# Weight loads move from SyncE's queue to GpSimd's, GpSimd's compute to VectorE: a hybrid attention and RWKV-7 decoder step

## The chip, the cores and the metric

One NeuronCore of a Trainium2 chip runs the whole program in one launch. The metric is the device time of one execution in microseconds (us); three executions of the kernel before took 3533.83, 3536.41 and 3536.74 us, and their median, 3536.41 us, is the time that the change is compared with.

Engine names as in the profile: PE is TensorE, PEld its weight loads, DVE is VectorE, ACT is ScalarE, POOL is GpSimd, SP is SyncE. SP does no arithmetic here: it only issues DMAs, one after another, each when the semaphores that it waits for have come.

## The reference, cut to what matters

One decoder layer (DEPTH is 1) and a final norm, for a prompt of 2048 tokens and for 8 samples of 8 new tokens with a cache of 2048 keys and values each. All inputs are float32, the model width is 1024.

```python
sh1, sc1, gt1, sh2, sc2, gt2 = ada_modulation(c, w_ada, b_ada)
h = rms_norm(x, norm1_g) * (1.0 + sc1) + sh1
proj = h @ w_in                               # 1024 -> 3*512 + 1792 columns
# first 1536 columns: q, k, v of 8 heads; dilated sliding windows (128,1), (512,4), (2048,16)
# other 1792 columns: token shift and low-rank parts, then the RWKV-7 recurrence of 8 heads
mix = concat([att, rw], -1) @ w_out           # 1024 -> 1024
x = x + gt1 * mix
h2 = rms_norm(x, norm2_g) * (1.0 + sc2) + sh2
x = x + gt2 * (square(relu(h2 @ w_ff1)) @ w_ff2)   # 1024 -> 4096 -> 1024
y = rms_norm(x, normf_g)
```

The outputs are y of both groups, the new keys and values, the RWKV states and the last projected rows.

## The kernel before

**Products.** Every large product is made in three passes (`mm3`, L311): weights and activations are each split into a high part, rounded to the matmul's type, and a rest (`split`, L256: ACT writes the high part on L258, DVE the rest on L259), and PE accumulates high times high, high times rest and rest times high in one PSUM tile.

**Weights.** A weight block of 512 KB is loaded into a staging tile named `stg`, split from there into a high and a low tile, and used by PE. `w_in` (L327) makes two such loads for each of 52 blocks of the input projection; `wload` (L1317) makes one for each block of the output projection (`w_out`) and of the feed-forward (`w_ff1`, `w_ff2`). The pools hold two `stg` tiles (three in the pool of the last token group), so a load can start only when the split of the load two before it has ended. Two other loads use the same `stg` tiles: parts of `w_ada` during the second stage (`ada_load`, L210) and the attention output that is read back from DRAM (`mlp_mix`, L1336). Every one of these loads is issued by SP.

**Stages.** The prompt is cut in four windows of 512 tokens. For each there is an input projection (i0 to i3, `in_stage`), an RWKV window (r0 to r3, `rwkv_window`) and an attention window (a0 to a3, `att_load`, `att_scores`, `att_values`); the samples have their own (s). Then five token groups go through output projection and feed-forward (m, p, f). Projections and feed-forward are dense PE work; the RWKV and attention windows are chains of small steps, and the kernel lets the two kinds run beside each other.

**Order.** A planner orders the instructions: `ORDER` (L37) gives each stage a start and an end in planned microseconds, from which each instruction gets a priority, and a scheduler with a cost model (`PlanCosts`, L1613) simulates the engines and fixes the order on each engine's queue. On the chip each queue then runs strictly in that order, and an instruction that has to wait holds up all that stands behind it on its queue.

**RWKV.** For each of 16 chunks of 128 tokens (and once for the samples) `rw_solve` (L676) inverts small triangular matrices. It goes through DRAM twice: `dA` is written (L687), read back into `sol` (L695), solved by DVE on L703 and L709, written as `dT` (L712), and read back in pieces (L716, L720, L721), all on SP. POOL clears `sol` before (L696 to L699). `rw_chunk` (L746) carries the state on: POOL multiplies the old state by the decay (L770), DVE adds the new part (L790, L791). The decay factors `DC` are picked out of `Dt` by six small POOL copies for each chunk (L862), and by two for the samples (L1166).

**Cached keys.** `att_load` (L920) reads queries and keys back from DRAM (`qt`, L934, on SP), transposes and splits them. From the second window on it also loads the transposed keys of the earlier windows from `kTd` into `kT`, which has one buffer (L931, POOL's queue: 12 loads, four for each window, of 512, 1024 and 1536 KB).

What else is on POOL's queue: one load of a constant (L466) and small constants at the start. Apart from L931 and L466 every DMA of the kernel is on SP.

Of the kernel before, what the change touches and what calls it, by code (L numbers as in the profile page):

```python
# [9 lines left out]
F32 = mybir.dt.float32  # L10
# [3 lines left out]
ALU = mybir.AluOpType  # L14
# [108 lines left out]
class Step:  # L123
# [203 lines left out]
    def w_in(self, c0, G):  # L327
        nc = self.nc
        tag = f"w{self.nwb % 2}"
        self.nwb += 1  # L330
        lo = G.tile([128, KD, 256], F32R, name="wlo", tag=tag)
        hi = G.tile([128, KD, 256], F32R, name="whi", tag=tag)
        for h in range(2):
            sl = slice(128 * h, 128 * h + 128)
            sg = G.tile([128, KD, 128], F32, name="stg", tag="stg")
            src = self.I["w_in"][0][:, c0 + 128 * h:c0 + 128 * h + 128]
            nc.sync.dma_start(sg, src.rearrange("(k p) c -> p k c", p=128))
            self.split(hi[:, :, sl], lo[:, :, sl], sg)
        return hi, lo

# [146 lines left out]
    def rw_load(self, V, g, r0, n, tag):  # L487
        nc = self.nc
        if g >= 0:
            raw = V.tile([128, n, 129], F32, name="raw", tag=tag)  # L490
            src = self.Pd[r0:r0 + n * 128]
            t0 = g * 128
            if g == 0:
                nc.gpsimd.memset(raw[:, :, 0:1], 0.0)
                nc.sync.dma_start(raw[:, :, 1:129], src[:, 0:128].rearrange("(k p) t -> p k t", p=128))
            else:
                nc.sync.dma_start(raw, src[:, t0 - 1:t0 + 128].rearrange("(k p) t -> p k t", p=128))
            return raw[:, :, 0:128], raw[:, :, 1:129]
        raw = V.tile([128, n, 8, 9], F32, name="raws", tag=tag)
        for k in range(n):  # L500
            rs = slice(r0 + k * 128, r0 + (k + 1) * 128)
            nc.sync.dma_start(raw[:, k, :, 1:9], self.Ps[rs].rearrange("p (b i) -> p b i", i=8))
        nc.vector.tensor_copy(raw[:, :, :, 0], self.shT[:, r0 // 128:r0 // 128 + n])
        return raw[:, :, :, 0:8], raw[:, :, :, 1:9]
# [171 lines left out]
    def rw_solve(self, V, psv, r, nch):  # L676

        nc = self.nc
# [14 lines left out]
        E = sol[:, 512:512 + 32 * nu].rearrange("p (u j) -> p u j", j=32)  # L693
        TZ = sol[:, 0:32 * nu].rearrange("p (u j) -> p u j", j=32)
        nc.sync.dma_start(sol[:, 0:256], dA.rearrange("u b h s t -> (u b h) (s t)")[None].to_broadcast([R, L, 256]))  # L695
        nc.gpsimd.memset(sol[:, 256:384], 0.0)  # L696
        for g in range(2):
            nc.gpsimd.memset(sol[64 * g:64 * g + 64, 256 + g:384:18], 1.0)
        nc.gpsimd.memset(E[64:128], 0.0)  # L699
        for s in range(15):  # L700
            m, n = 15 - s, s // 2 + 1
            t3 = tmp[:, 0:m * n].rearrange("p (j i) -> p j i", i=m)
# [43 lines left out]
    def rw_chunk(self, V, psv, r, c, nxt, po):  # L746
        nc = self.nc
        F, F1, bkT, AT, AO, UV, DC = (r[k] for k in ("F", "F1", "bkT", "AT", "AO", "UV", "DC"))
        unit = lambda h: (c * 2 + h % 2) * 4 + h // 2
        Fh = lambda h: (F1 if h % 2 else F)[:, h // 2, c]  # L750
        odd = lambda t, q: t.rearrange("p (k q) e -> p q k e", q=2)[:, q]
        px = psv.tile([128, 4, 64], F32, name="px", tag="c")
        for h in range(8):
            o = 64 * (h % 2)
            nc.tensor.matmul(
                px[o:o + 64, h // 2], Fh(h)[:, 0:64], UV[:, c, h], start=True, stop=True, tile_position=(0, o)
            )
        for h in range(8):
            o = 64 * (h % 2)
            nc.tensor.matmul(  # L760
                po[o:o + 64, h // 2, 64 * c:64 * c + 64], UV[:, c, h], Fh(h)[:, 64:128],
                start=c == 0 and h < 2, stop=False, tile_position=(0, o),
            )
        xs = V.tile([128, 8, 64], F32, name="xs", tag="xs")
        x4 = xs.rearrange("p (q k) e -> p q k e", q=2)
        s0 = xs[0:64]
        for q in range(2):
            nc.vector.tensor_copy(x4[64:128, q], px[64 * q:64 * q + 64])
        dcb = DC[0:64, c, :, None].to_broadcast([64, 8, 64])
        nc.gpsimd.tensor_tensor(s0, UV[0:64, c], dcb, op=ALU.mult)  # L770
        pu = psv.tile([128, 4, 64], F32, name="pu", tag="c")
        for h in range(8):
            o = 64 * (h % 2)
            nc.tensor.matmul(
                pu[o:o + 64, h // 2], AT[64:128, unit(h)], x4[64:128, h % 2, h // 2],
                start=True, stop=True, tile_position=(64, o),
            )
        for q in range(2):
            nc.scalar.activation(odd(UV[0:64, c], q), pu[64 * q:64 * q + 64], AF.Copy)
        ps = psv.tile([128, 4, 64], F32, name="psS", tag="c")  # L780
        for h in range(8):
            o = 64 * (h % 2)
            nc.tensor.matmul(
                ps[o:o + 64, h // 2], bkT[:, c, (h % 2) * 4 + h // 2], UV[:, c, h],
                start=True, stop=True, tile_position=(0, o),
            )
        for q in range(2):
            o = slice(64 * q, 64 * q + 64)
            dq = DC[o, c].rearrange("p (k q) -> p q k", q=2)[:, q, :, None].to_broadcast([64, 4, 64])
            nc.vector.tensor_tensor(odd(nxt, q), ps[o], dq, op=ALU.mult)  # L790
        nc.vector.tensor_tensor(nxt, nxt, s0, op=ALU.add)  # L791
        for h in range(8):
            o = 64 * (h % 2)
            nc.tensor.matmul(  # L794
                po[o:o + 64, h // 2, 64 * c:64 * c + 64], UV[0:64, c, h], AO[:, unit(h)],
                start=False, stop=c == 1 and h >= 6, tile_position=(0, o),
            )
# [46 lines left out]
    def rwkv_window(self, w, V, psv):  # L844
# [8 lines left out]
        for g in range(g0, g0 + 4):  # L853
# [5 lines left out]
            for par in range(2):  # L859
                for c in range(2):  # L860
                    for o in (0, 64) if par else (0,):
                        nc.gpsimd.tensor_copy(  # L862
                            DC[o:o + 64, c].rearrange("p (k q) -> p k q", q=2)[:, :, par],
                            r["Dt"][64 * par:64 * par + 64, :, 64].rearrange("p (k c) -> p k c", c=2)[:, :, c],
                        )
# [54 lines left out]
    def att_load(self, w, hp, V, psv):  # L920
# [7 lines left out]
        qs1 = V.tile([128, 2, 512], F32R, name="qs1", tag="qs")  # L928
        ql1 = V.tile([128, 2, 512], F32R, name="ql1", tag="ql")
        if w > 0:  # L930
            nc.gpsimd.dma_start(kT[:, :, :, 0:w], self.kTd[hp][:, :, :, 0:w])  # L931
        for src in (self.qd[t0:t0 + TS, cs], kwin[t0:t0 + TS, cs]):
            qt = V.tile([128, 4, 128], F32, name="qt", tag="qt")
            nc.sync.dma_start(qt, src.rearrange("(i p) c -> p i c", p=128))  # L934
# [147 lines left out]
    def rwkv_sample(self, V, psv):  # L1082
# [80 lines left out]
                nc.vector.tensor_tensor(xo[:, :, 1], po, xo[:, :, 1], op=ALU.add)  # L1163
        DC = V.tile([64, 8, 8], F32, name="DCs", tag="DCs")
        for par in range(2):
            nc.gpsimd.tensor_copy(  # L1166
                DC.rearrange("p b (k q) -> p k q b", q=2)[:, :, par],
                r["Dt"][64 * par:64 * par + 64, :, 8].rearrange("p (k b) -> p k b", b=8),
            )
# [147 lines left out]
    def wload(self, src, n, G):  # L1317
# [1 line left out]
        nc = self.nc  # L1319
        nk = 1024 // n  # L1320
        sg = G.tile([128, nk, n], F32, name="stg", tag="stg")
        nc.sync.dma_start(sg, src.rearrange("(k p) c -> p k c", p=128))
        hi = G.tile([128, nk, n], F32R, name="wh", tag="wh")
        lo = G.tile([128, nk, n], F32R, name="wl", tag="wl")
        self.split(hi, lo, sg)
# [364 lines left out]
```

## Time and profile before

| | |
|---|---|
| median of three runs | 3536.41 us (3533.83 to 3536.74) |
| the profiled execution's own time | 3537.64 us |
| its span, first to last instruction | 3535.6 us |
| mean granted TensorE clock, share of full speed | 0.96 |
| busy: PE, PEld | 3305.4 us, 2811.1 us |
| busy: DVE, ACT, POOL | 2208.6 us, 1711.1 us, 92.8 us |
| DMA: moved, mean rate | 496.54 MB, 140 GB/s |

Busy time is time in which an engine carried out instructions, waits not counted. The granted clock is what the chip allowed TensorE: 1.0 is 2.4 GHz and 0.5 is 1.2 GHz. The chain that ended last is followed back from the last instruction, at each step to what released it. In it a piece "DMA a<-b" runs from the issue of that transfer to its landing. The DMA queue that belongs to SP is called hardware_dynamic in the profile, POOL's software_dynamic.

### The profile page before, as it was taken

Reading aid. Unit: us, or ns where it says so; the run is one execution under the profiler, and the core shown is the slowest. Engines: PE = TensorE matmul, PEld = TensorE weight load, DVE = VectorE, ACT = ScalarE, POOL = GpSimd, SP = SyncE. Lnnn points to the kernel's source line nnn. Section 1 sums busy time; section 2 is a strip of 40 time slices with the busy share of each in tenths; the row PEclk is TensorE's granted clock in tenths of the full one; section 3 lists DMA queues with packets and bytes.
Section 4 is the critical chain, followed back from the end, with each engine's and each line's share of the span. In section 5 each row is a group of like instructions: output and inputs, shape, how many; then the busy total and the mean of one; then the engine's idle time right before and its main releaser. Section 6 shows DMA issues by size and latency. Waiting matters only on the chain.

```text
span 3535.6 us, 66399 instructions
## 1 busy us (share of the span) xinstructions
PE 3305.4 (93%) x26546; PEld 2811.1 (80%) x26546; DVE 2208.6 (62%) x4872; ACT 1711.1 (48%) x3156; POOL 92.8 (3%) x219
## 2 busy tenths in 40 slices
PE   6999999888899999999999999889999997979998
PEld 4887988788888777788877786776777776869998
DVE  4565655635677676787766566543665877756666
ACT  4455444545455465556544542443554545444453
POOL 0000000000000000000000000000000000000000
PEclk8999999998989999999999999999999998989999
DMA  7456645334353443355354244978543335345464
GB/s 242 143 152 198 202 128 149 104 89 105 94 148 107 130 114 89 103 140 180 86 145 120 81 97 117 277 229 239 146 119 93 93 87 172 101 148 155 156 185 155
DMA packets 731756, 496.54 MB, mean 140 GB/s; under 512 B 126134, under 2 KB 682344, under 8 KB 731448
## 3 DMA queue, kind: packets, MB, share of 16 engines
q1 hardware_dynamic: 718824, 479.65, 47.2%
q0 software_dynamic: 12624, 12.65, 1.5%
q8 instruction: 209, 3.42, 0.4%
q14 instruction: 99, 0.81, 0.1%
HBM read 424.11 MB, written 63.77 MB: 138 GB/s over the span
## 4 chain that ended last, share of the span: by engine, by line
PE 80%; DMA 8%; ACT 5%; DVE 5%; issue 1%; SPq 0%; ACTq 0%; DVEq 0%
PE mmps L317 19%; PE mmps L315 19%; PE mmps L316 19%; PE pops L1047 2%; PE aps L652 2%; PE ptps L1057 2%; DMA stg<-in_w_out_dram 1%; DMA kst<-in_cache_k_dram 1%; DMA out_dram<-pev 1%; DMA stg<-in_w_in_dram 1%; PE ktps L1231 1%; DVE wl L259 1%; PE yps L729 1%; PE ops L794 1%; PE lps L551 1%
## 5 line engine op out<-in xcount | busy, mean ns | idle before, releaser
L258 ACT ACTIVATE wh<-stg 128x1024 fp32r<-128x1024 f32 x384 | 406.1, 1058 | 588.8 <-PE mmps L316 489.8
L315 PE MATMUL mmps<-h2hi,wh 128*128 128x256 f32 (+2 forms) x1864 | 630.6, 339 | 28.2 <-ACT wh L258 17.4
L259 DVE TENSOR_TENSOR wl<-stg,wh 128x1024 fp32r<-128x1024 f32 x384 | 470.6, 1226 | 274.1 <-ACT wh L258 259.6
L317 PE MATMUL mmps<-h2hi,wl 128*128 128x256 f32 (+2 forms) x1864 | 630.9, 339 | 8.6 <-DVE wl L259 8.4
L316 PE MATMUL mmps<-h2lo,wh 128*128 128x256 f32 (+2 forms) x1864 | 629.2, 338 | 1.4 <-DVE h2lo L304 1.4
L315 PE MATMUL mmps<-hid,wh 128*128 128x512 f32 (+2 forms) x1280 | 459.8, 360 | 3.5 <-DVE h L284 1.8
L317 PE MATMUL mmps<-hid,wl 128*128 128x512 f32 (+2 forms) x1280 | 460.7, 361 | 0.1
L316 PE MATMUL mmps<-hid,wh 128*128 128x512 f32 (+2 forms) x1280 | 459.4, 359 | 0.0
L315 PEld LDWEIGHTS mmps<-h2hi,wh 128*128 128x128 f32 x1864 | 362.1, 194 | 58.6 <-ACT wh L258 18.4
L317 PEld LDWEIGHTS mmps<-h2hi,wl 128*128 128x128 f32 x1864 | 361.4, 194 | 39.8 <-DVE wl L259 10.7
L316 PEld LDWEIGHTS mmps<-h2lo,wh 128*128 128x128 f32 x1864 | 361.9, 194 | 29.3 <-DVE h2lo L304 2.2
L315 PEld LDWEIGHTS mmps<-hid,wh 128*128 128x128 f32 x1280 | 243.3, 190 | 34.5 <-issue 4.0
L317 PEld LDWEIGHTS mmps<-hid,wl 128*128 128x128 f32 x1280 | 243.5, 190 | 33.4 <-issue 5.1
L316 PEld LDWEIGHTS mmps<-hid,wh 128*128 128x128 f32 x1280 | 243.5, 190 | 28.7 <-issue 0.8
L1302 DVE SCALAR_TENSOR_TENSOR acc<-mmps,ada,acc 128x512 f32<-128x512 f32 (+1 forms) x280 | 179.3, 642 | 133.5 <-PE mmps L317 131.9
L315 PE MATMUL mmps<-whi,hhi 128*128 128x256 f32 (+1 forms) x816 | 234.2, 287 | 0.0
L317 PE MATMUL mmps<-whi,hlo 128*128 128x256 f32 (+1 forms) x816 | 233.9, 287 | 0.0
L316 PE MATMUL mmps<-wlo,hhi 128*128 128x256 f32 (+1 forms) x816 | 233.7, 286 | 0.0
L315 PE MATMUL mmps<-hhi,whi 128*128 128x512 f32 (+2 forms) x608 | 216.5, 358 | 13.0 <-ACT pev L393 6.5
L316 PE MATMUL mmps<-hlo,whi 128*128 128x512 f32 (+2 forms) x608 | 215.0, 354 | 1.1 <-DVE hlo L304 1.1
L317 PE MATMUL mmps<-hhi,wlo 128*128 128x512 f32 (+2 forms) x608 | 214.6, 353 | 0.0
L259 DVE TENSOR_TENSOR wlo<-stg,whi 128x1024 fp32r<-128x1024 f32 x104 | 126.6, 1228 | 93.1 <-ACT whi L258 92.6
(345 smaller groups left out, 5904.3 us busy)
## 6 DMA issues: line engine op xcount, KB each, us to landing
stg<-in_w_ff_dram SPq DMA_DIRECT2D x320, 512.0 KB
stg<-in_w_in_dram SPq DMA_DIRECT2D x104, 512.0 KB
stg<-in_w_out_dram SPq DMA_DIRECT2D x64, 512.0 KB
kst<-in_cache_k_dram SPq DMA_DIRECT2D x80, 256.0 KB
vst<-in_cache_v_dram SPq DMA_DIRECT2D x80, 256.0 KB
xt<-in_x_prompt_dram SPq DMA_DIRECT2D x32, 512.0 KB
wada<-in_w_ada_dram SPq DMA_DIRECT2D x32, 512.0 KB
Pd<-pev SPq DMA_DIRECT2D x56, 256.0 KB
```

Of the source, the lines that this page charges most:

```text
L258: nc.scalar.activation(hi, src, AF.Copy)
L259: nc.vector.tensor_tensor(lo, src, hi.bitcast(F32), op=ALU.subtract)
L315: nc.tensor.matmul(out, wh(k), xh(k), start=k == 0, stop=False)
L316: nc.tensor.matmul(out, wh(k), xl(k), start=False, stop=False)
L317: nc.tensor.matmul(out, wl(k), xh(k), start=False, stop=k == nk - 1)
L551: nc.tensor.matmul(pt[:, hp], self.wa2[lo:lo + 64, hp * 128:(hp + 1) * 128], src[lo:lo + 64, 0], start=True, stop=True,)
L652: nc.tensor.matmul(pt[:, hp], bk[o:o + 64, hp, c], F[o:o + 64, hp, c], start=True, stop=True)
L729: nc.tensor.matmul(pz[q, u], x, y, start=True, stop=True, tile_position=(64 + o, 64 + o))
L794: nc.tensor.matmul(po[o:o + 64, h // 2, 64 * c:64 * c + 64], UV[0:64, c, h], AO[:, unit(h)], start=False, stop=c == 1 and h >= 6, tile_pos ...
L1047: nc.tensor.matmul(out[o:o + 64], v[:, o:o + 64], pT[:, j], start=j0 + j < 2, stop=j0 + j >= len(jobs) - 2, tile_position=(0, o),)
L1057: nc.tensor.transpose(pt[:, j], jb[j][0], self.ident)
L1302: nc.vector.scalar_tensor_tensor(o, pt[:, 0:np_], gt[:, ob, 0:1], o, op0=ALU.mult, op1=ALU.add)
```

## The change

The two places that issue weight loads, `w_in` and `wload`, issue them from POOL's queue. The 12 loads of cached keys, which were on POOL, go to SP, each as two loads of 64 partitions, as plain float32. All that POOL computed (memsets on L494, L696, L698 and L699, copies on L862 and L1166, the product on L770) is given to DVE. The loads of `w_ada` and of the attention output, which share the `stg` tiles, stay on SP. The planner runs again on the changed program.

```diff
--- before.py
+++ after.py
@@ -334,7 +334,7 @@
             sl = slice(128 * h, 128 * h + 128)
             sg = G.tile([128, KD, 128], F32, name="stg", tag="stg")
             src = self.I["w_in"][0][:, c0 + 128 * h:c0 + 128 * h + 128]
-            nc.sync.dma_start(sg, src.rearrange("(k p) c -> p k c", p=128))
+            nc.gpsimd.dma_start(sg, src.rearrange("(k p) c -> p k c", p=128))
             self.split(hi[:, :, sl], lo[:, :, sl], sg)
         return hi, lo
 
@@ -491,7 +491,7 @@
             src = self.Pd[r0:r0 + n * 128]
             t0 = g * 128
             if g == 0:
-                nc.gpsimd.memset(raw[:, :, 0:1], 0.0)
+                nc.vector.memset(raw[:, :, 0:1], 0.0)
                 nc.sync.dma_start(raw[:, :, 1:129], src[:, 0:128].rearrange("(k p) t -> p k t", p=128))
             else:
                 nc.sync.dma_start(raw, src[:, t0 - 1:t0 + 128].rearrange("(k p) t -> p k t", p=128))
@@ -693,10 +693,10 @@
         E = sol[:, 512:512 + 32 * nu].rearrange("p (u j) -> p u j", j=32)
         TZ = sol[:, 0:32 * nu].rearrange("p (u j) -> p u j", j=32)
         nc.sync.dma_start(sol[:, 0:256], dA.rearrange("u b h s t -> (u b h) (s t)")[None].to_broadcast([R, L, 256]))
-        nc.gpsimd.memset(sol[:, 256:384], 0.0)
+        nc.vector.memset(sol[:, 256:384], 0.0)
         for g in range(2):
-            nc.gpsimd.memset(sol[64 * g:64 * g + 64, 256 + g:384:18], 1.0)
-        nc.gpsimd.memset(E[64:128], 0.0)
+            nc.vector.memset(sol[64 * g:64 * g + 64, 256 + g:384:18], 1.0)
+        nc.vector.memset(E[64:128], 0.0)
         for s in range(15):
             m, n = 15 - s, s // 2 + 1
             t3 = tmp[:, 0:m * n].rearrange("p (j i) -> p j i", i=m)
@@ -767,7 +767,7 @@
         for q in range(2):
             nc.vector.tensor_copy(x4[64:128, q], px[64 * q:64 * q + 64])
         dcb = DC[0:64, c, :, None].to_broadcast([64, 8, 64])
-        nc.gpsimd.tensor_tensor(s0, UV[0:64, c], dcb, op=ALU.mult)
+        nc.vector.tensor_tensor(s0, UV[0:64, c], dcb, op=ALU.mult)
         pu = psv.tile([128, 4, 64], F32, name="pu", tag="c")
         for h in range(8):
             o = 64 * (h % 2)
@@ -859,7 +859,7 @@
             for par in range(2):
                 for c in range(2):
                     for o in (0, 64) if par else (0,):
-                        nc.gpsimd.tensor_copy(
+                        nc.vector.tensor_copy(
                             DC[o:o + 64, c].rearrange("p (k q) -> p k q", q=2)[:, :, par],
                             r["Dt"][64 * par:64 * par + 64, :, 64].rearrange("p (k c) -> p k c", c=2)[:, :, c],
                         )
@@ -928,7 +928,8 @@
         qs1 = V.tile([128, 2, 512], F32R, name="qs1", tag="qs")
         ql1 = V.tile([128, 2, 512], F32R, name="ql1", tag="ql")
         if w > 0:
-            nc.gpsimd.dma_start(kT[:, :, :, 0:w], self.kTd[hp][:, :, :, 0:w])
+            for o in (0, 64):
+                nc.sync.dma_start(kT[o:o + 64, :, :, 0:w].bitcast(F32), self.kTd[hp][o:o + 64, :, :, 0:w])
         for src in (self.qd[t0:t0 + TS, cs], kwin[t0:t0 + TS, cs]):
             qt = V.tile([128, 4, 128], F32, name="qt", tag="qt")
             nc.sync.dma_start(qt, src.rearrange("(i p) c -> p i c", p=128))
@@ -1163,7 +1164,7 @@
                 nc.vector.tensor_tensor(xo[:, :, 1], po, xo[:, :, 1], op=ALU.add)
         DC = V.tile([64, 8, 8], F32, name="DCs", tag="DCs")
         for par in range(2):
-            nc.gpsimd.tensor_copy(
+            nc.vector.tensor_copy(
                 DC.rearrange("p b (k q) -> p k q b", q=2)[:, :, par],
                 r["Dt"][64 * par:64 * par + 64, :, 8].rearrange("p (k b) -> p k b", b=8),
             )
@@ -1319,7 +1320,7 @@
         nc = self.nc
         nk = 1024 // n
         sg = G.tile([128, nk, n], F32, name="stg", tag="stg")
-        nc.sync.dma_start(sg, src.rearrange("(k p) c -> p k c", p=128))
+        nc.gpsimd.dma_start(sg, src.rearrange("(k p) c -> p k c", p=128))
         hi = G.tile([128, nk, n], F32R, name="wh", tag="wh")
         lo = G.tile([128, nk, n], F32R, name="wl", tag="wl")
         self.split(hi, lo, sg)
```

## Rows read from the trace of the kernel before

**Rows 1.** The page, parts 1 and 4: busy time of the engines; the chain by engine.

```profile
PE 3305.4 (93%) x26546; PEld 2811.1 (80%) x26546; DVE 2208.6 (62%) x4872; ACT 1711.1 (48%) x3156; POOL 92.8 (3%) x219
...
PE 80%; DMA 8%; ACT 5%; DVE 5%; issue 1%; SPq 0%; ACTq 0%; DVEq 0%
```

**Rows 2.** Busy time by stretch, from:to, length; then clock, DMA share, GB/s.

```profile
0.00:100.00 100.00, 69.19 (x424) 52.24 (x425) 40.43 (x99) 44.91 (x80) 2.15 (x12) 0.86 0.71 235
700.00:1000.00 300.00, 257.02 (x2387) 237.21 (x2388) 149.77 (x441) 131.58 (x289) 11.91 (x34) 0.89 0.41 98
2200.00:2500.00 300.00, 261.26 (x2309) 214.44 (x2310) 146.40 (x267) 125.88 (x212) 0.87 (x1) 0.93 0.85 241
2900.00:3200.00 300.00, 252.30 (x2373) 227.92 (x2373) 197.03 (x412) 140.59 (x258) 8.40 (x19) 0.86 0.46 135
3200.00:3500.00 300.00, 300.00 (x2295) 299.41 (x2295) 201.33 (x332) 141.29 (x209) 0.00 (x0) 1.00 0.56 170
```

**Rows 3.** The tile stg: count, duration in ns (least, median, most), first and last.

```profile
L258 ACT ACTIVATE wh<-stg x384: 1039/1060/1070, 984.8 to 3510.0; 128x1024 fp32r<-128x1024 f32 x192
...
L337 SPq DMA_DIRECT2D stg<-in_w_in_dram x104: 367/383/7537, 19.5 to 895.0; - x104
```

**Rows 4.** Waits of SP's queue and of ACT: us in total, times, longest.

```profile
SPq L1322 <- DVE wl L259: 887.8, 228, 15.3
...
ACT wh L258 <- DMA stg<-in_w_ff_dram: 45.3, 23, 6.5
```

**Rows 5.** The chain in order of time: start, length, what; weight loads in it.

```profile
21.03 11.52 DMA stg<-in_w_in_dram
...
359.35 3.94 DMA stg<-in_w_in_dram
...
644.90 4.64 DMA stg<-in_w_in_dram
...
1018.50 5.20 DMA stg<-in_w_out_dram
...
3139.91 4.64 DMA stg<-in_w_out_dram
...
3146.98 5.64 DMA stg<-in_w_ff_dram
```

**Rows 6.** The same chain: other transfers in it, right behind weight loads on SP.

```profile
773.04 12.33 DMA raw<-Pd
...
1199.40 7.98 DMA qt<-out_dram
...
1444.55 6.57 DMA sol<-dA
...
1807.85 5.07 DMA qt<-qd
```

**Rows 7.** The same chain: the load of cached keys in it.

```profile
2487.86 11.11 DMA kT<-kTd
```

**Rows 8.** POOL's loads of keys: duration in ns; by size, median us to landing.

```profile
L931 POOL DMA_DIRECT2D kT<-kTd x12: 873/873/955, 1198.1 to 2631.6; - x12
...
kT<-kTd POOLq DMA_DIRECT2D x4, 1536.0 KB, 8.7
...
kT<-kTd POOLq DMA_DIRECT2D x4, 512.0 KB, 4.9
```

**Rows 9.** Groups by form on POOL: busy us, mean ns, idle before, releasers.

```profile
L770 POOL TENSOR_TENSOR xs<-UV,DC 64x512 f32<-64x512 f32 x32 | 34.4, 1075 | 472.8 <-DVE UV L791 449.5 <-PE mmps L316 9.4 <-DVE sol L709 6.8
L862 POOL COPY DC<-Dt 64x4 f32<-64x4 f32 x96 | 29.6, 318 | 657.8 <-ACT Dt L566 585.5 <-DMA stg<-in_w_ff_dram 69.7
```

**Rows 10.** Groups by form on DVE, the nearest to what is moved there.

```profile
L791 DVE TENSOR_TENSOR UV<-UV,xs 64x512 f32<-64x512 f32 x28 | 19.0, 679 | 0.9
...
L736 DVE MEMSET AT<- 32x512 f32 x16 | 7.8, 485 | 2.5 <-issue 0.5 <-DVE bv L674 0.3 <-DVE xs L768 0.2
...
L1014 DVE COPY m<-swps 128x8 f32<-128x8 f32 x16 | 2.6, 163 | 7.6 <-PE swps L914 7.6
```

## The prediction

> **What bounds the kernel now.** I read the page first. PE is busy 93% of the span and takes 80% of the chain; DMA has 8% of the chain, ACT and DVE 5% each, and SP's queue itself 0% [rows 1]. So PE's work sets the time, and a change of queues can only win or lose what PE stands idle: 3535.6 - 3305.4 = 230 us. The table by stretch says where that is: 30.8 us in the first 100, 43.0 us from 700 to 1000, 38.7 us from 2200 to 2500 and 47.7 us from 2900 to 3200, and none from 3200 to 3500 [rows 2]. The clock goes with it: 0.86 to 0.93 in the stretches with idle PE, 1.00 in the last one, so an idle microsecond that goes can bring a little more than itself. DMA bandwidth is near its end only from 2200 to 2500 (share 0.85).
>
> Then the weight loads: 384 + 104 = 488 of 512 KB, whose issue holds SP for about 0.38 us each [rows 3]. SP stood 887.8 us, 228 times, before weight loads until DVE had split the block before, 3.9 us each time, and this is a quarter of the span [rows 4]. The weights themselves are not late by that, since SP stands ready when the buffer comes free; what is late is what stands behind them on SP. ACT, in turn, waited for landings only 23 times, 45.3 us, in the feed-forward.
>
> In the chain of waits I counted the weight loads: nine of `w_out`, five of `w_in` and one of `w_ff`, 15 pieces; undisturbed they land in 3.94 to 5.6 us [rows 5]. Four other pieces were issued by SP right behind a weight load that had waited: 12.33, 7.98, 6.57 and 5.07 us [rows 6]. Last, one load of cached keys from POOL, 11.11 us [rows 7].
>
> **The change, term by term,** against the profiled execution's own 3537.64 us (2 us around its span); the median of the runs is 1.2 us lower, which I take off at the end.
>
> *a. Weight loads from POOL: 0, from -10 to +14 us.* The nearest row is POOL's own load of 512 KB: 4.9 us from issue to landing, 0.87 us of it on POOL [rows 8]. Against SP's shortest, 3.94, that is +0.96 for each of the 15 pieces, +14 us; against the longer ones (5.20, 5.64) it is -0.3 to -0.7, at most -10 us for all. I take 0, since the 4.9 lies in the middle of what SP's pieces show. POOL's time is no bound: 488 x 0.87 = 425 us, 12% of the span, on a queue that has nothing else left. With SP's 488 x 0.38 = 185 us of issuing gone nothing is won, for SP is not in the chain.
> One rule speaks against this move. The row shows POOL taking 873 to 955 ns for each of its 12 loads, with DVE busy 62% of the span: it was never held long. The Trainium skill, "SBUF — State Buffer", section "SBUF: two separate sides", says that a DVE instruction in a two-port mode locks GpSimd out while GpSimd writes DMA descriptors, so that the transfer waits for DVE. By the rows the sum has nothing for it; by the rule each load could wait for one DVE instruction, which the rivals price.
>
> *b. SP freed: -15, from 0 to -45 us.* If the four pieces behind weight loads fell to 3.94 us, they would give 31.95 - 4 x 3.94 = 16 us; I take half, 8, since other work ends almost as late (PE goes on under several of them). Off the chain: each of 17 solves makes five dependent trips through SP (`dA` out and in, `dT` out and in, `AT` in). A trip meets a weight wait with the quarter above and then loses half of 3.9 us: 17 x 5 x 0.25 x 1.95 = 41 us of RWKV latency. PE idles 15% in the stretches at 700 and 2900 (90.7 of 600 us), so some 7 us of it would show. Bound below: nothing; above: half of those 90.7 us, 45. What is late next is the store or the split that the same chunk waits for.
>
> *c. Cached keys over SP: -2, from -2.4 to +6 us.* The piece of 11.11 us against the median of its size, 8.7, is -2.4; two halves of 64 partitions one after the other would be 2 x 8.7 - 11.1 = +6. Twelve pairs now wait in SP's queue for the one `kT` buffer; behind them stand `qt`, the values and the solve's trips. At the 3.9 us of a weight wait that is 47 us of standing, against 888 that go, so I keep the gain of b.
>
> *d. POOL's compute on DVE: +4, from -1 to +9 us.* 32 products of L770 (now 1.075 us on POOL) and 96 copies of L862 [rows 9] become DVE instructions like L791, 0.679 us, and L1014, 0.163 us; 17 large memsets like L736, 0.485 us; and 57 smaller ones at 0.163 [rows 10]: 21.7 + 15.6 + 8.2 + 9.3 = 55 us on DVE. DVE's share of the chain is 177 of 2208.6 busy us, 8%: +4. Above: 17% of the time lies in the two stretches with idle PE at 700 and 2900, +9; below: 32 x 0.4 us shorter products, 8% of it, -1. If the PE work that covers them is gone, as at 2900, each of the two products of a chunk adds its 0.68 us to the recurrence.
>
> *e. The first 45 us: 0, from -8 to +8 us.* On SP the first `w_in` loads stood behind eight loads of `w_ada` and landed at 32.5 (21.03 + 11.52). On POOL nothing is before them. Some 2 MB more then run beside `w_ada`, which PE needs first; 1 MB more took a key load from 4.9 to 8.7 us, so 2 MB cost up to 8 us. The same 2 MB split early free ACT and DVE later: two landings of 4 us less.
>
> The planner also gets other costs and may order the engines anew; no row prices that, and it stays inside the bounds. Sum: 0 - 15 - 2 + 4 + 0 = -13: 3524.6, and on the runs' median 3523 us. With all lower ends (-10 - 45 - 2.4 - 1 - 8 = -66) it is 3470, with all upper ends (14 + 0 + 6 + 9 + 8 = 37) 3573.
>
> **The rivals.**
> *Slower: landings.* Weights land 0.96 us later everywhere; the place is ACT's queue, where a split that waits holds up PSUM evacuations behind it. Price: 14.4 us on the chain's 15 pieces and 22 us on ACT's 23 waits, with the upper ends of c and d (8 + 5 more): 3523 + 49 = 3572. It decides against b and c once the pieces land about 0.9 us later each. For it: 3.94 against 4.9 in the rows; against it: ACT's wait for landings is small, and PE is full from 3200 on although weights run at 170 GB/s there.
> *No change.* The four pieces are long for another reason, the transfer itself or a full DMA, and not for SP's order; then b and c are nothing and d stays: 3540. For it: SPq has 0% of the chain; against it: 12.33 us for one piece where a weight load of 512 KB can land in 3.94. The Trainium skill, "DMA: Bandwidth & Descriptors", section "Issuing engines are not separate DMA queues", says the same of all queues: one set of 16 engines, and a second issuer saves only the time of issuing. The rows bear it out from 2200 on only (share 0.85).
> *The lock.* Each of those 15 + 23 landings waits in addition for a DVE instruction of 0.485 us: +18, 3541. Row for row the 12 POOL loads speak against it.
> *More.* RWKV windows get as short as b's end allows, the idle PE at 700 and 2900 halves: 3493.
>
> **How the numbers follow.** Forecast 0.40, more 0.10, no change 0.13, lock 0.05, slower landings 0.32. About 0.2%, 7 us, is what a measurement of this kernel can tell from no change. So faster 0.50, same 0.18 (no change and lock), slower 0.32. The likeliest case alone spans 3500 to 3529. The range takes in both outer cases and the bounds: 3470 to 3580.
>
> **What would show it.** In the changed profile: a for right if POOL's weight loads last about 0.87 us and land near 5 us, wrong if over 6; b if SP's largest waits are no longer weights, the piece `raw<-Pd` after 770 is near 4 us or gone, and PE is busier from 700 to 1000 and 2900 to 3200; c if no `kT` piece over 9 us is in the chain; d if DVE's busy time grows by some 55 us and its share of the chain stays near 5%; e if the first dense PE work begins within 8 us of before. The forecast is wrong if ACT's wait for `stg` landings doubles, or if PE's idle time moves without shrinking.

## The result, and the profile after

The changed kernel takes **3649.2 us** (median of 6 runs, 3641.2 to 3677.7) against 3536.6 for the kernel before, measured beside it: 1.0317 times, 95% interval 1.0279 to 1.0354. The forecast was 3523 us, and the time lies above the whole range. It is slower by 113 us, and the sign is that of the rival "slower: landings". The profiled execution has a span of 3639.5 us, 104 more than that of before.

The page of the changed kernel, parts 1 and 3 (busy time of the engines; DMA queues with packets, MB and share of 16 engines):

```profile
PE 3340.2 (92%) x26546; PEld 2835.0 (78%) x26546; DVE 2251.1 (62%) x5074; ACT 1713.5 (47%) x3156; POOL 411.2 (11%) x493
...
q0 software_dynamic: 70416, 255.95, 24.7%
q1 hardware_dynamic: 305896, 236.35, 23.6%
```

PE still sets the time. Beside [rows 1] it stands idle 299 us (3639.5 - 3340.2) instead of 230, which is 69 of the 104; the other 35 are PE's own instructions, which last longer. DVE took over 43 us of work, not the 55 of the forecast. Half of the bytes now go through POOL's queue at the same price, 0.096% of the engines' span per MB against 0.100% on SP's queue, so the bytes are not what became dearer.

The same stretches as in [rows 2], of the changed kernel (clock, DMA share and GB/s are the last three columns; the work in a stretch has shifted by up to 100 us):

```profile
0.00:100.00 100.00, 66.83 (x412) 50.41 (x413) 41.22 (x106) 44.09 (x79) 11.52 (x17) 0.86 0.67 225
700.00:1000.00 300.00, 253.97 (x2367) 235.67 (x2366) 157.40 (x478) 133.58 (x292) 19.43 (x22) 0.89 0.46 94
2200.00:2500.00 300.00, 253.80 (x2138) 201.61 (x2136) 155.08 (x297) 113.55 (x195) 25.10 (x29) 0.90 0.73 211
2900.00:3200.00 300.00, 265.07 (x2567) 227.52 (x2565) 213.73 (x487) 142.33 (x272) 31.76 (x38) 0.88 0.40 112
3200.00:3500.00 300.00, 267.59 (x1888) 260.63 (x1887) 176.00 (x304) 129.14 (x195) 62.59 (x76) 0.95 0.52 155
```

What 700 to 1000 and 2200 to 2500 had of idle PE is still there (46 us in each, against 43 and 39); from 2900 to 3200 13 us are gone, and the last stretch, which was full, has 32 us of idle PE. Much of both is a shift: the last token group begins at 3120 us in the kernel before and at 3214 in the changed one, and the idle time around its start, 23.7 us from 3100 to 3200 before, is 24.1 us from 3200 to 3300 now. What is new there is the 8.3 us from 3300 to 3500.

What ACT waits for, first in the changed kernel, then the two groups of the kernel before that [rows 4] leave out (us in total, times, longest):

```profile
ACT wh L258 <- DMA stg<-in_w_ff_dram: 101.5, 44, 6.5
...
ACT wh L258 <- DMA stg<-in_w_out_dram: 64.5, 41, 4.4
...
ACT whi L258 <- DMA stg<-in_w_in_dram: 45.5, 18, 5.3
```

```profile
ACT wh L258 <- DMA stg<-in_w_out_dram: 30.8, 20, 4.3
...
ACT whi L258 <- DMA stg<-in_w_in_dram: 28.6, 18, 4.4
```

With the 45.3 us of [rows 4], ACT's waits for landed weights were 104.7 us; now they are 211.5. That is the sign which the prediction gave for being wrong. SP, in turn, was freed, and this is what it does with the time (its largest waits in the changed kernel):

```profile
SPq L687 <- DVE AT L655: 222.2, 15, 43.8
SPq L396 <- ACT pev L393: 220.0, 44, 13.0
SPq L1466 <- PE mmps L317: 185.0, 5, 154.2
SPq L980 <- PE ptps L1058: 182.4, 8, 35.1
```

No weight is among them. SP stands in front of the next transfer in its order, whose producer isn't ready. Of the prediction's signs, the one for *a* came true as well (POOL's loads land 4.7 to 5.6 us after their issue, medians): it tells how late a load is, but not what that costs.

### The profile page after: what moved, and what is told of

Its sections match the earlier page's. It is cut to its first block, busy times and chain, and to the rows that moved or that the text cites. A ratio compares the mean times of both kernels' runs of the same rounds, so it can differ in the third digit from the quotient of the medians.

```text
span 3639.5 us, 66426 instructions
## 1 busy us (share of the span) xinstructions
PE 3340.2 (92%) x26546; PEld 2835.0 (78%) x26546; DVE 2251.1 (62%) x5074; ACT 1713.5 (47%) x3156; POOL 411.2 (11%) x493
## 4 chain that ended last, share of the span: by engine, by line
PE 46%; DMA 11%; issue 5%; ACT 4%; DVE 4%; POOL 0%; SPq 0%; ACTq 0%; POOLq 0%; DVEq 0%
PE mmps L315 10%; PE mmps L316 10%; PE mmps L317 10%; DMA stg<-in_w_ff_dram 3%; DMA stg<-in_w_out_dram 3%; DMA kst<-in_cache_k_dram 2%; PE pops L1048 2%; PE ptps L1058 2%; ACT wh L258 1%; DVE wl L259 1%; PE aps L652 1%; PE ktps L1232 1%; DMA x2d<-xt 1%; DMA stg<-mixd 1%; DMA qt<-qd 1%
## 5 line engine op out<-in xcount | busy, mean ns | idle before, releaser
L315 PE MATMUL mmps<-h2hi,wh 128*128 128x256 f32 (+2 forms) x1864 | 639.8, 343 | 48.2 <-ACT wh L258 32.7
L316 PE MATMUL mmps<-h2lo,wh 128*128 128x256 f32 (+2 forms) x1864 | 636.5, 341 | 1.2 <-DVE h2lo L304 1.0
L1323 POOL DMA_DIRECT2D stg<-in_w_ff_dram x320 | 261.9, 819 | 1895.2 <-DVE wl L259 1461.8
```

The costliest lines, as they stand in the source:

```text
L315: nc.tensor.matmul(out, wh(k), xh(k), start=k == 0, stop=False)
L316: nc.tensor.matmul(out, wh(k), xl(k), start=False, stop=False)
L1323: nc.gpsimd.dma_start(sg, src.rearrange("(k p) c -> p k c", p=128))
```

## The experiments

Two theories stood at first. **Landing theory:** a load issued from POOL lands later, ACT's split waits, and the evacuations behind it in ACT's queue hold up PE. **Order theory:** the planner, given other queues, put all engines into another order, and that costs. Each alteration of this kernel gives a new order, so changing one part alone and planning anew cannot tell the two apart. Most runs therefore keep an order: the program is planned twice, and the second time each instruction gets an edge to the one that stood before it on its engine in the first plan. Such an edge costs no semaphore; PE, ACT and what does not move then have line for line the order of the first plan. Below, ORDER_OF and ENGINES (QUEUE where the weights alone move) name the queues of the first and of the second plan. The code is cut at the dots.

```diff
+    nc, _ = program(ENGINES, program(ORDER_OF)[1])
...
+    for name in order:
+        for ins in place.get(name, ()):
+            key = str(ins.engine)
+            if key in last:
+                tc.add_manual_dep(
+                    ins, last[key], mybir.DependencyInfo(mybir.DependencyClass.NoSync, mybir.DependencyReason.DATA), reason="pin"
+                )
+            last[key] = ins.name
```

**Weights alone: two queues, two orders.** Apart from the code that holds the order, only L337 and L1322 differ from the kernel before, which in w_pool and w_pool_oldorder come to this:

```diff
-        nc.sync.dma_start(sg, src.rearrange("(k p) c -> p k c", p=128))
+        nc.gpsimd.dma_start(sg, src.rearrange("(k p) c -> p k c", p=128))
```

> The kernel before with the 488 weight loads alone issued from POOL; the planner orders all engines anew. Landing theory (the loss is that the loads land later and ACT's splits wait): most of the loss is here, 1.020 to 1.032 of before, ACT's waits for landed weights near the 211 us of the changed kernel against 105 before. Order theory (the loss is the planner's new order, not the queue): any value, 0.995 to 1.03, since the order is new here too. Compute theory (the loss is the work moved onto DVE): 0.995 to 1.005.

> As w_pool, but each engine keeps exactly the order of instructions that it has in the kernel before (edges between neighbours that cost no semaphore). Landing theory: as slow as w_pool within 0.5%, 1.015 to 1.03. Order theory: 0.993 to 1.004, faster or equal, because only the issuing queue differs from before.

> Weights on SP as before, but every engine in the order that the planner gave w_pool, SP's and POOL's shares merged in that order. Landing theory: near before, 0.995 to 1.006. Order theory: 1.01 to 1.03, the time goes with the order. SP then has weight loads in an order made for two queues, so a value over w_pool's would be that.

Measured, with the kernel before beside it at 3539.0 us:

| | order of before | order planned for POOL |
|---|---|---|
| weights on SP | 3539.0 | 3629.1, 1.0255 (1.0236 to 1.0273) |
| weights on POOL | 3598.2, 1.0169 (1.0150 to 1.0188) | 3647.0, 1.0312 (1.0285 to 1.0338) |

Both theories hold, and neither alone: the queue costs 59 us at the old order, the new order 90 us with weights on SP and 49 with weights on POOL. The two costs do not add up (59 + 90 against 108). A likely reason, not tried by itself: the new order was made for a free SP, so that holding SP with weights costs more in it.

With the order held, the two traces can be laid over each other. ACT's waits in w_pool_oldorder (as above), and the same instructions of ACT in the kernel before and in w_pool_oldorder (start, length, what, in brackets the idle time before and what ended it):

```profile
ACT wh L258 <- DMA stg<-in_w_ff_dram: 98.0, 43, 5.6
...
ACT wh L258 <- DMA stg<-in_w_out_dram: 63.4, 33, 5.0
...
ACT whi L258 <- DMA stg<-in_w_in_dram: 40.3, 19, 6.8
```

```profile
1063.18 1.06 ACT L258 ACTIVATE wh<-stg 128x1024 fp32r<-128x1024 f32 x1 [0.46 <-DMA stg<-in_w_ff_dram]
1064.14 0.48 ACT L590 ACTIVATE sq<-xx,oka,cols 128x128 f32<-128x128 f32 x1
1064.95 0.47 ACT L1304 ACTIVATE acc<-mmps,ada 128x256 f32<-128x256 f32 x1 [0.33 <-PE mmps L317]
1065.60 1.06 ACT L258 ACTIVATE wh<-stg 128x1024 fp32r<-128x1024 f32 x1 [0.17 <-DMA stg<-in_w_ff_dram]
...
1069.84 1.06 ACT L258 ACTIVATE wh<-stg 128x1024 fp32r<-128x1024 f32 x1
```

```profile
1087.61 1.06 ACT L258 ACTIVATE wh<-stg 128x1024 fp32r<-128x1024 f32 x1 [1.21 <-DMA stg<-in_w_ff_dram]
1088.57 0.48 ACT L590 ACTIVATE sq<-xx,oka,cols 128x128 f32<-128x128 f32 x1
1088.96 0.45 ACT L1304 ACTIVATE acc<-mmps,ada 128x256 f32<-128x256 f32 x1
1090.84 1.06 ACT L258 ACTIVATE wh<-stg 128x1024 fp32r<-128x1024 f32 x1 [1.43 <-DMA stg<-in_w_ff_dram]
...
1097.74 1.06 ACT L258 ACTIVATE wh<-stg 128x1024 fp32r<-128x1024 f32 x1 [2.60 <-DMA stg<-in_w_ff_dram]
```

In the first of each, 0.46 us of waiting became 1.21; in the second 0.17 became 1.43; the third did not wait at all and now waits 2.60. From the first of these splits to the third ACT takes 10.1 us instead of 6.7. So a delay of under a microsecond makes waits out of loads that had a little slack, and delays add up where one split follows the next, since with two buffers the next load is issued only after the split before last.

Subtracting the start of each of PE's 26546 matmuls in one trace from that of the same matmul in the other shows where the time goes (worked out from the two traces; the first line is the place in the kernel before):

```
at (us)         50    700    800   1050   1100   1550   1750   2200   2250   2800   3250   3350   3500
later by (us)  5.8   14.5   19.8   22.0   29.9   28.3   37.2   34.8   45.1   50.6   63.0   71.8   71.8
```

Much of the loss, 46 of the 71.8 us, comes in steps at the stage starts (0 to 50, 700 to 760, 1040 to 1080, 1580 to 1600, 2230 to 2270) and shortly before the last group's feed-forward (3250 to 3320), where fresh weights are wanted at once; from 1100 to 1550 and 1750 to 2200 nothing is lost. Two small gains are in it as well, -2.3 us between 760 and 800 and -2.8 us between 1200 and 1250, at the places of the pieces `raw` and `qt` of [rows 6] that stood on SP behind weight loads. PE's busy time in this run is 3331.8, so of 71.8 us 45 are idle PE and 26 longer instructions, with a granted clock of 0.952 against 0.960. The profiled execution, at 3609.2 us, was 11 us above the median of its four, so 71.8 us stand here for the 59 of the medians.

**The suspected delay doubled.** Ahead of each weight load POOL clears three quarters of the buffer that the load then fills; nothing else differs from w_pool_oldorder (LATE is 1 in the second plan; L337 shown, L1322 is changed alike).

```diff
-            nc.sync.dma_start(sg, src.rearrange("(k p) c -> p k c", p=128))
+            nc.gpsimd.memset(sg[:, 0:3 * sg.shape[1] // 4], 0.0) if LATE else None; getattr(nc, WQ).dma_start(sg, src.rearrange("(k p) c -> p k c", p=128))
```

> w_pool_oldorder (every engine in the order of before) with one POOL memset of three quarters of the staging buffer ahead of each weight load, so that each lands some 0.8 to 1.0 us later still; this doubles the suspected cost. Landing theory: the loss grows at least in step, from 1.017 to 1.033 or more, up to 1.05, since loads with a little slack turn into waits too. Rival (the loss comes from POOL's way of moving the data, contention on the DMA engines or with DVE, and not from when a load lands): 1.014 to 1.022 as before the memset.

Measured: 3659.7 us, 1.0335 (1.0299 to 1.0372): 115 us over before, where one delay gave 59. ACT's waits rise with it:

```profile
ACT wh L258 <- DMA stg<-in_w_ff_dram: 148.4, 61, 6.1
ACT wh L258 <- DMA stg<-in_w_out_dram: 100.8, 45, 5.7
...
ACT whi L258 <- DMA stg<-in_w_in_dram: 56.3, 27, 6.1
```

105, 202 and 306 us of waiting (before, w_pool_oldorder, w_pool_later) go with 0, 59 and 115 us of loss. The loads themselves land as in w_pool_oldorder (median 4.7 us from issue in the feed-forward), they only start later: from the release of the buffer to the issue it takes 1.10 us (median) instead of 0.29, so 0.80 us more on top of the 0.9 that POOL's queue costs by itself. So the time at which a load lands is a cause of the right size, and nothing else in how POOL moves data is needed for it.

**Compute on VectorE**, first planned anew, then in the order of before. The edit is the change's own, with weights left on SP and keys on POOL; so in L494, L696 to L699, L862 and L1166, as here in L770:

```diff
-        nc.gpsimd.tensor_tensor(s0, UV[0:64, c], dcb, op=ALU.mult)
+        nc.vector.tensor_tensor(s0, UV[0:64, c], dcb, op=ALU.mult)
```

> Only POOL's compute instructions go to VectorE; weights stay on SP, cached keys on POOL; the planner orders anew. Compute theory: 1.005 to 1.02, DVE 43 us busier and the recurrence longer by it. Landing theory: 1.000 to 1.003, 4 us as forecast. Order theory: 0.995 to 1.02, with no relation to the 43 us.

> As compute_dve, but PE, ACT, SP and the rest of DVE keep exactly the order of the kernel before. Order theory (compute_dve's 36 us are its new order): 1.000 to 1.004, the forecast's 4 us. Compute theory (the 43 us on DVE lie on the recurrence): 1.007 to 1.013, as compute_dve.

Measured: planned anew 3574.7 us, 1.0101 (1.0080 to 1.0122); in the order of before 1.0010 (0.9994 to 1.0027). The moved work costs about 4 us, as forecast, though the interval does not tell that from nothing; the rest of compute_dve's 36 us is its new order. The run also shows that holding an order costs next to nothing by itself.

**Cached keys over SP**, in the order of before (the change's own edit is shown; the run's is written otherwise and issues the same):

```diff
-            nc.gpsimd.dma_start(kT[:, :, :, 0:w], self.kTd[hp][:, :, :, 0:w])
+            for o in (0, 64):
+                nc.sync.dma_start(kT[o:o + 64, :, :, 0:w].bitcast(F32), self.kTd[hp][o:o + 64, :, :, 0:w])
```

> The cached keys alone go to SP as two halves, every engine in the order of before. Forecast (term c): 0.998 to 1.002. Held-queue theory (the halves wait in SP's queue for the kT buffer, and the solve's trips stand behind them): 1.004 to 1.012, with SP standing some 50 us or more before those loads.

Measured: 1.0052 (1.0035 to 1.0070), some 18 us by the ratio (12.5 between the medians) and over the forecast's bound of 6. The place is the start of an attention window. SP's queue in the kernel before, then SP and PE in keys_oldorder (timeline around 2490):

```profile
2486.41 0.52 SPq L934 DMA_DIRECT2D qt<-qd  x1
2487.27 0.37 SPq L934 DMA_DIRECT2D qt<-out_dram  x1
```

```profile
2494.09 2.10 SPq L931 DMA_DIRECT2D kT<-kTd  x2
2496.25 0.61 SPq L934 DMA_DIRECT2D qt<-qd  x1
```

```profile
2507.68 1.09 PE L937 MATMUL qtps<-ident,qt 128*128 128x128 f32 x4 [8.53 <-DMA qt<-qd]
```

In the kernel before POOL issued the keys at 2487.86 [rows 7], 1.45 us after `qt`. On one queue the two halves, 1.5 MB, go first; `qt` is used 11.4 us after its issue, and PE stands 8.53 us before its first transpose. The laid-over traces have +5.7 us at 1810 and +7.8 us at 2490, most of the whole. SP being held was not it: it stood 39.6 us in 9 waits before key loads, but without a step in PE's time there. The changed kernel has the same piece in its chain, where the kernel before had `kT` with 11.11 us [rows 7]:

```profile
2551.13 15.18 DMA qt<-qd
```

**The whole change in the order of before:**

```diff
+ORDER_OF, ENGINES = ('sync', 'gpsimd', 'gpsimd', 0), ('gpsimd', 'vector', 'sync', 1)
```

The four stand for the queue of the weights, POOL's compute, the queue of the keys, and whether these go in halves.

> All three parts of the change, with every engine in the order of the kernel before. Two-cause theory (later landings plus a worse order): the landings of w_pool_oldorder remain and little else, 1.015 to 1.022; the 40 us up to the changed kernel are the order. Parts theory (the new order does nothing by itself, compute and keys cost the rest): 1.027 to 1.034.

Measured: 1.0208 (1.0187 to 1.0228). The three parts at that order give 1.0169 + 0.0052 + 0.0010 = 1.0231, the same within the intervals. From 1.0208 to 1.0317 the rest, about 1.1%, is the new order.

**Is the new order forced, or chance?** Four plans with another price of a DMA start and nothing else changed, two of each kernel (2250 or 2400 ns), and a fifth, change_told, in which only POOL's price is raised.

```diff
-    ACCESS, DMA, CYCLE = 105, 2300.0, 0.443
+    ACCESS, DMA, CYCLE = 105, 2250.0, 0.443
...
-        T.DMA_START_FIXED_NS, T.PE_CYCLE = self.DMA, self.CYCLE
+        T.DMA_START_FIXED_NS, T.PE_CYCLE = self.DMA, self.CYCLE; T.DMA_START_POOL_CYCLES_SWDGE = 1600.0
```

> The kernel before with nothing changed on the chip but the planner's price of a DMA start, 2250 for 2300 ns: 1216 lines of difference in PE's order, where the changed kernel has some thousands. Luck theory (the order of before is a picked one, and any other costs about 1%): 1.006 to 1.02. Theory of a misled planner (only an order planned for weights on POOL, as if they landed as early as SP's, is bad): 0.997 to 1.004.

> The kernel before, planned with 2400 ns for 2300; nothing else differs. Luck theory: away from 1.000 by 0.4% or more, 0.99 to 1.015. Theory that only the change's orders are bad: 0.997 to 1.004, as replan_2250's 0.998.

> The changed kernel, planned with 2250 for 2300 ns per DMA start on every queue; nothing else differs. Luck theory: it lands away from 1.032 by 0.4% or more, either way, 1.02 to 1.04. Theory that the change itself forces a bad order: 1.029 to 1.035.

> The changed kernel, planned with 2400 for 2300 ns per DMA start. Scatter theory: somewhere from 1.018 to 1.04, and away from 1.032 by 0.4% or more. Theory that the change forces a worse order: 1.026 to 1.034, like the three plans so far (1.026, 1.030, 1.032) and above the 1.021 of the order of before.

> The changed kernel, where the planner's price of a DMA start on POOL is raised by 900 of its cycles (0.75 us), so that it plans with loads about as late as they are. Misled-planner theory (the new order is bad since it was made for loads that land as early as SP's): back to change_oldorder, 1.015 to 1.024. Luck theory (orders scatter by about 1%, whatever they assume): 1.022 to 1.04.

Measured: the kernel before at 2250 0.9976 (0.9954 to 0.9999), at 2400 1.0075 (1.0044 to 1.0106); the changed kernel at 2250 1.0256 (1.0202 to 1.0311), at 2400 1.0302 (1.0274 to 1.0330), told POOL's delay 1.0297 (1.0263 to 1.0332). So plans of one and the same kernel differ by up to 1%, and telling the planner that POOL's loads are later does not mend its order: the theory of the misled planner falls. That the order of before is a picked optimum falls as well, since 2250 is no worse. All four plans of the changed kernel lie above its 1.0208 in the order of before, the nearest with an interval that takes it in. With four plans it stays open whether that is chance or whether the freed SP leads the planner into worse orders; compute_dve shows that an order alone can cost 0.9% with weights on SP.

**Slack or count.** Only the feed-forward's 320 loads go to POOL (L1322 for `w_ff`, order of before).

> Only the feed-forward's 320 loads are issued from POOL, projections stay on SP; order of before. Slack theory: the feed-forward's loads mostly have slack, and half of the rise of ACT's waits was theirs (54 of 98 us), so 1.003 to 1.009. Theory by count (each POOL load costs alike): 320/488 of 59 us = 39 us, 1.010 to 1.013.

Measured: 1.0069 (1.0037 to 1.0102), by the ratio 24 us (20 between the medians) of the 59 for two thirds of the loads. The value is that of the slack theory; the interval just touches the other. By the difference, not by a run of their own, the 168 loads of the projections, which come in bursts at the stage starts, cost the larger part. ACT's waits do not share out the loss, however, as that expectation had it:

```profile
ACT wh L258 <- DMA stg<-in_w_ff_dram: 113.0, 56, 5.7
```

Against the 45.3 us of [rows 4] that is 68 us more waiting, as much as 70% of the rise in w_pool_oldorder, for some 40% of its loss. 90.4 of the 113.0 us lie behind 3136 us, where the last group begins. So a microsecond of ACT's waiting seems to cost less there than at the stage starts, and the sum of the waits is a sign of the loss, not its price.

**A third staging buffer,** in one plan for both queues; room comes from one `F1` buffer of the last RWKV window.

```diff
-    MG = dict(h2h=1, h2l=1, acc=1, wh=3, wl=3, stg=2, hid=NHID, st=4, rlu=2)
+    MG = dict(h2h=1, h2l=1, acc=1, wh=3, wl=3, stg=3, hid=NHID, st=4, rlu=2)
```

> The kernel before with a third staging buffer in the feed-forward pool (room comes from one F1 buffer less in the last RWKV window), planned anew for SP's queue. It is the control for stg3_POOL. Its plan is new, so by itself 0.99 to 1.015 of before.

> As stg3_SP, in exactly stg3_SP's order of every engine, with the 488 weight loads issued from POOL. Landing theory: from the first feed-forward on a load can be issued one split earlier, so its 0.9 us are mostly hidden; the loss against stg3_SP falls from 59 us to 20 to 40 us, and to under 17 us (from 34) between the first and the fourth output projection. Rival (POOL's way of moving the data costs, whatever the lead): 50 to 65 us in all, over 28 in that stretch.

Measured: stg3_SP 3884.3 us, 1.0962 (1.0939 to 1.0986), stg3_POOL 3915.1, 1.1058. As a kernel this is far slower, and the forecast for the control was far off: its first split of an output projection's weights comes at 1550.8 us, where [rows 3] have it at 984.8, and the last group begins 346 us later than in the kernel before; that the larger pool found room only then is likely, but was not followed up. As a comparison of queues it tells something, for both runs have one order. POOL loses 31 us to SP instead of 59, and from the first group's load of `mixd` to the fourth's only 2.4 (1681.1 us against 1683.5). ACT's waits for the feed-forward and the output projection, stg3_SP, then stg3_POOL:

```profile
ACT wh L258 <- DMA stg<-in_w_out_dram: 18.3, 17, 3.4
...
ACT wh L258 <- DMA stg<-in_w_ff_dram: 0.3, 1, 0.3
```

```profile
ACT wh L258 <- DMA stg<-in_w_out_dram: 49.3, 24, 5.6
...
ACT wh L258 <- DMA stg<-in_w_ff_dram: 6.8, 6, 2.1
```

In the feed-forward, where a load has one split more of lead, the delay makes next to no waits; in the output projection's bursts it still does, 31 us more. Of the loss, +21.9 us are there by 650, in the input projection, which kept two buffers. The order is another here than in the kernel before, so these two runs alone do not show that the buffer did it. w_pool_oldorder bears it out in the order of before: the pool of its last group has three `stg`, and from 3390 us on, where 62 splits lie and nearly all matmuls are this group's, ACT waits for a weight load only twice, 1.8 us in all. A kernel clearly faster than before did not come out of these runs; the best is replan_2250, by 0.24% (0.01 to 0.46).

## Why the prediction was wrong, point by point

Two terms of the sum failed: the weight loads, taken at 0, cost 59 us, and the planner's new order, put at nothing because no row priced it, came with some 39 more. The premise of the working, that a change of queues can only win or lose what PE stands idle, failed too: 35 of the 104 us are longer PE instructions, at a granted clock of 0.948 instead of 0.960.

*a. Weight loads from POOL, 0 (-10 to +14): measured +59 at the held order.* This is the step that failed. The delay per load was right: 4.9 against 3.94 us [rows 5, 8]. In the laid-over traces the time from the release of the buffer to the split that waits for it rises from 4.3 to 5.2 us in the feed-forward and from 5.5 to 6.4 in the output projection (medians of the loads that were waited for), of which 0.27 is POOL reacting later to the release (0.29 against 0.03 us) and about 0.5 its longer issue. Two things were wrong. SP's longer pieces were taken to cancel the delay (4.9 "lies in the middle"), but they get it on top, as the output projection shows. And the count: only the 15 pieces of the chain were priced, and ACT's 23 waits in the rival. The chain is one path. ACT waited for 61 weight loads in the kernel before (the 23 of the feed-forward, for which the prediction has "only 23 times", and 38 of the projections) and for 95 in w_pool_oldorder. In the trace of before about 135 of the 488 loads are split less than 6 us after their issue (29 of `w_in`, 41 of `w_out`, some 65 of `w_ff`), so they had less than about 2 us of slack against SP's 3.94. Counting loads by slack would have shown that far more than 15 or 38 were at stake; what each of them costs it would not have shown.
The Trainium skill, "DMA: Bandwidth & Descriptors", section "Latency and other measured facts", gives a first byte after about 1 us for loads from GpSimd and 0.6 for the others. That points the right way, with 0.4 of the 0.9 us seen here.

*b. SP freed, -15: about -5 of it is seen.* At the places of the pieces `raw` and `qt` PE gains 2.3 and 2.8 us at the held order, in part because they are issued sooner. But these two were not long because of SP's order. With no weight load on SP `raw` still takes 11.21 us from issue to landing, not the 3.94 that the sum gave it, and the `qt` of 1199 us is used 7.7 us after its issue instead of 8.1; for these the rival "no change" had the reason right. In the chain of w_pool_oldorder:

```profile
793.74 11.21 DMA raw<-Pd
```

The 888 us of standing [rows 4] turned into standing in front of producers, for SP keeps its order; the 41 us of RWKV latency did not show.

*c. Keys over SP, -2 (-2.4 to +6): +18 at the held order.* The prediction saw that `qt` would stand behind the keys, but priced only SP's waiting for the buffer (47 us, set against 888), not the time that the 1.5 MB themselves take in front of it.

*d. Compute on DVE, +4 (-1 to +9): right as far as can be told,* 1.0010 (0.9994 to 1.0027), with 43 us more on DVE.

*e. The first 45 us, 0 (-8 to +8): inside,* +5.8 us by 50 in w_pool_oldorder, none of it a gain.

*The planner's new order, "inside the bounds": wrong,* some 39 us (1.0317 against 1.0208), more than the 37 of all upper ends together; whether the change forces it stays open.

*The rivals.* "Slower: landings" had the mechanism and the place (ACT's queue, evacuations behind a waiting split). Its 36 us for landings are too small by 23, with 95 loads that waited and not 38; its 3572 has no term for the order. The condition in it, "once the pieces land about 0.9 us later", is met. "The lock": the 488 loads hold POOL 0.75 to 1.03 us each with DVE busy 62% of the span, so no run here shows the lock-out that the Trainium skill, "SBUF — State Buffer", section "SBUF: two separate sides", describes. "No change" by the rule of the Trainium skill that all queues share one set of engines: the trace agrees in the bytes' price (0.096% of the engines' span per MB on POOL's queue, 0.100% on SP's), but the rule says nothing of when a load starts, and this decided.

## What to carry to other kernels

Price a later landing by the slack of every load (issue to first use), not by the pieces of one chain, and expect the bursts at stage starts, where two buffers give no lead, to pay most; take the waits that result as a sign, not as the price. Where a planner orders the engines, hold its order to see what a queue costs, and plan the same kernel a few times to see what an order costs: here both were about 1 to 2%. A queue that is freed gains only what was ready and stood behind the wait; and what shares a queue goes in its order, so a short load should not follow a long one.

## What the runs showed that was not expected

The same 512 KB cost SP's queue far more packets than POOL's. Between the kernel before and w_pool_oldorder nothing but the queue of 488 loads differs; the hardware queue has 718824 - 293224 = 425600 packets fewer, 872 per load on the average or some 600 bytes each, and the software queue 82896 - 12624 = 70272 more, 144 per load or 3.6 KB each. By the sizes in the two traces SP's queue moves such a block in packets of 512 bytes or 1 KB, one for each row piece of the source, and POOL's in 128 packets of 4 KB, one for each partition (335872 packets of 512 bytes and 81920 of 1 KB are gone from SP's queue, 62464 of 4 KB are new on POOL's); on either queue 16 packets of 4 bytes come with a load. The time on the 16 engines per MB is nearly the same, so the packets' number did not matter here. Part 3 of the page, first of the kernel before, then of w_pool_oldorder:

```profile
q1 hardware_dynamic: 718824, 479.65, 47.2%
q0 software_dynamic: 12624, 12.65, 1.5%
```

```profile
q0 software_dynamic: 82896, 268.53, 26.9%
q1 hardware_dynamic: 293224, 223.77, 21.9%
```

And 26 of the 72 us that w_pool_oldorder's profiled execution loses are not idle time: PE's instructions of the same number and order last longer, at a granted clock of 0.952 instead of 0.960. The clock goes with the idle time in the changed kernel too: from 3300 to 3500 PE is idle 8.3 us at 1.00, from 3200 to 3300, around the last group's start, 24.1 us at 0.85.
